# A float32 encoder layer on one core: its FFN from two token halves with paired down products to an up phase over all tokens and a down phase

## The chip, the core and the metric

One core of a Trainium2 chip runs the whole layer. The metric is the device time of one execution in microseconds. TensorE (PE) multiplies, VectorE (DVE), ScalarE (ACT) and GpSimd (POOL) work on tiles in SBUF, SyncE (SP) issues most DMAs.

## The reference, cut to what matters

Two inputs, 1024 and 256 tokens of width 1024, pass through the same layer; the kernel lays them one behind the other, T = 1280. Attention, a recurrent branch, a memory branch and their gates give `merged`; the part that the change touches begins there:

```python
x = x + merged @ w_out                       # part_out
h = rmsnorm(x, ffn_norm)
u = dwconv3(h @ w_up, ffn_conv) + ffn_conv_b # 1024 -> 2 x 2816, convolution of 3 tokens
u_val, u_gate = jnp.split(u, 2, axis=-1)
y = x + (jax.nn.silu(u_gate) * u_val) @ w_down   # 2816 -> 1024
return rmsnorm(y, final_norm)
```

`dwconv3` mixes each token with its two neighbours and takes zeros beyond the ends of each of the two inputs.

## The kernel before, in words

**Precision.** Every operand of the large products is split in two: a high half, cast on ACT (L182), and a low half, the difference, taken on DVE or POOL (L183). A product is three matmul passes, high by high, low by high, high by low.

**Projection.** `part_merge` writes `merged` transposed into the tile `hT`; `part_out` multiplies it with w_out tile by tile (ten tiles of 128 tokens), adds x (L1197), takes the norm (L233 to L253), scales (L1145, `xn`), transposes on TensorE (L1148) and keeps the result, transposed, as the FFN's input. The first five tiles' sums stay in SBUF (`acc`), the last five go to DRAM (`X2`, `XT`).

**FFN.** It runs over two halves of 640 tokens. Within a half the loop is over f, 22 blocks of 128 hidden columns; block f has a value part and a gate part. `products` (L1483) computes both parts by one level of Strassen's scheme, seven products in place of eight: the two parts by the two halves of the 1024 input rows by two token pieces of 322 columns. `ffn_weights` (L1344) makes the seven weight operands of an f: four raw blocks of w_up come by DMA (`wraw`), POOL forms sums (L1360, L1361, L1385, L1391), and `put` splits each into `fw`; it goes through all 22 f twice, once per half. Each product is 12 matmuls (L1520); its evacuation adds PSUM to earlier pieces (L1498 to L1510) and builds `fz`. `act` (L1527) then does the convolution: the centre tap on ACT (L1535), four side taps per half on DVE (L1542), Tanh on ACT, the gate step on DVE (L1547), the product on POOL (L1548), and splits the result into `fah` and `fal` (L1555, L1558). After every second f, `down` (L1560) multiplies two f with four pieces of w_down: ten PSUM tiles of six matmuls (L1574), each added by DVE into `acc` (L1565). `down_weights` splits w_down on POOL, for each half again. `finish` takes the last norm and stores. Operands of the second half are prepared during the first (`ffn_second`, `ffn_operands(1)`).

The order is written by hand: `hook(j)` after each product takes steps of the generators, and `in_order` (L1204) chains the instructions of PE, DVE, ACT and POOL in the order of the program within the FFN. The waiting chains are therefore those of the text:

```python
for f in range(22):
    products(half, f, hook)                 # 7 products of 12 matmuls, 322 columns
    if f % 2 and 3 <= f < 21:
        down(half, lambda t: act_steps(1))  # 10 tiles of 6 matmuls, 512 columns
```

PSUM has four buffers for up products (`psd`) and four for down products (`psw`). SP issues the loads in its own order; X2, XT and BT are stored from ACT's queue.

Of the kernel before, what the change touches and what calls it, by code (L numbers as in the profile page):

```python
# [32 lines left out]
AHEAD = 7  # L33

ACT_AFTER, DOWN_AFTER, BEHIND_AFTER = (1, 3, 5, 6), (0, 1, 5, 6), ((1, 3, 5), (1, 4))
ACT_STEPS = (2, 1, 1, 2, 2, 2, 1, 1, 1, 1)

SCALE_COLS = (1024,) * 5 + (0, 0, 512, 1024, 768)
# [28 lines left out]

CUT = 640

HALF = 322  # L70
IN_ORDER = (mybir.EngineType.PE, mybir.EngineType.DVE, mybir.EngineType.Activation, mybir.EngineType.Pool)

MTOK = (TOK, TOK, tuple((t, 320) for t in range(0, T, 320)))
# [81 lines left out]
class Builder:  # L155
# [136 lines left out]
    def build(self):  # L292
# [3 lines left out]
        with ExitStack() as ctx:  # L296
# [26 lines left out]
            mt, first = self.part_merge(mx)  # L323
            self.accp = ctx.enter_context(self.pool("acc"))

            self.acc = [self.accp.tile([128, D], F32, tag="acc", name="acc", bufs=5) for i in range(5)] + [None] * 5
            self.X2 = [None] * 5 + [self.dr.tile([128, D], F32, name="X2_%d" % i) for i in range(5, 10)]

            self.xp = ctx.enter_context(self.pool("xk"))
            self.zb = [self.xp.tile([128, 646], F32, name="fz%d" % i) for i in range(4)]  # L330
            self.xk = self.zb + [self.xp.tile([128, 646], F32, tag=t, name="xk", bufs=1) for t in ("fu0", "fu1", "fth")]
            self.xk.append(self.xp.tile([128, D], F32, tag="gain", name="xk", bufs=1))
            self.edge = self.xp.tile([128, 8, 2], F32, name="fedge")
            self.XT = self.dr.tile([128, 8, 640], F32, name="XT")
            self.BT = self.dr.tile([128, 28, HALF], F32, name="BT")
            self.raw_pool(ctx, "w", 5)

            self.fd = [self.H[:, c:c + 1024].rearrange("p (i n) -> p i n", i=2) for c in (0, 1024)]
            cols = [2048 + HALF * n for n in range(25)] + [8 * T + HALF * n for n in range(31)]
            b = [self.H[:, c:c + HALF] for c in cols]  # L340
            self.B = [[b[8 * j + 2 * k:8 * j + 2 * k + 2] for k in range(4)] for j in range(7)]
            self.W = []
            self.weights = self.ffn_weights()
            self.operands = self.ffn_operands(0)
            with wx, mx:
                self.part_out(mt, first)
            self.part_ffn()
# [715 lines left out]
    def part_merge(self, mx):  # L1063

        nc, a, dr = self.nc, self.ins, self.dr
        with self.pool("mg") as pool, self.pool("psm", 6, space=PSUM) as self.psd, ExitStack() as rx:
# [4 lines left out]
            mt = [[[self.H[:, c:c + CUT] for c in range(8 * CUT * i, 8 * CUT * (i + 1), CUT)] for i in (u, u + 1)] for u in (0, 2)]  # L1071
# [13 lines left out]
            def branch(n, m, o):  # L1085
# [4 lines left out]
                def evac(ps, t0, w):  # L1090
# [7 lines left out]
                    if n == 2:  # L1098
                        u, c = (0, t0) if t0 < CUT else (1, t0 - CUT)
                        h, l = mt[u][0][m][:, c:c + w], mt[u][1][m][:, c:c + w]  # L1100
# [19 lines left out]
        return mt, wh  # L1120
# [12 lines left out]
    def part_out(self, mt, first):  # L1133

        nc, a, pool = self.nc, self.ins, self.wo
        with self.pool("pso2", 2, space=PSUM) as psp, self.pool("psx", 2, space=PSUM) as pst, ExitStack() as rx:
            tmp = rx.enter_context(self.pool("ot"))
            new = lambda name: tmp.tile([128, D], F32, tag=name, name=name, bufs=1)
            ws = first + [self.out_rows(k, pool, "o%d" % k, 1) for k in range(2, 8)]

            def turn(i, x, junk):
# [7 lines left out]
                w = 128 if i < 5 else 2  # L1149
                if i < 6:  # L1150

                    for k in range(8):
                        for t0, t1, d in ((0, HALF, 0), (642 - HALF, 642, 2)):
# [30 lines left out]
            for i in range(10):  # L1184
# [4 lines left out]
                if i == 7:  # L1189
                    next(self.weights)  # L1190
# [489 lines left out]
```

## Time and profile before

| what | value |
|---|---|
| runs, median (lowest to highest) | 3241.52 us (3240.58 to 3250.91), 3 runs |
| the profiled execution | 3230.12 us, span 3227.9 us |
| mean granted TensorE clock | 0.958 |
| PE, DVE, ACT, POOL busy in the span | 2981.7, 2252.6, 1364.2, 1439.7 us |
| the FFN's last matmul, last instruction | 3216, 3227.9 us |

Busy times of engines overlap each other and are means over all stages; a busy PE also counts pipelined matmuls, so its dense pace is read from the starts of neighbouring matmuls. "PEclk" is the clock granted to TensorE as a share of the full one.

### The profile page before, as it was taken

The numbers are of one execution on the slowest core, as the hardware profiler recorded it, in microseconds if no ns is written. First come the engines' busy times: TensorE is split into PE (matmuls) and PEld (weight loads), VectorE is DVE, ScalarE is ACT, GpSimd is POOL, SyncE is SP. The second block draws the span as 40 slices with busy tenths as digits, with TensorE's granted clock in tenths as the row PEclk, the third lists the DMA queues.
The fourth block names the chain that finished last, engine by engine and source line by source line (L and its number), as shares of the span: only waits on it lengthen the run. The fifth ranks groups of instructions, "written<-read, shape, count | busy, mean of one in ns | idle before, by whom it ended". The sixth has DMA issues, their size and how long they took to land. (4 is left out here: it accounts for less than half of the span.)

```text
span 3227.9 us, 50384 instructions
## 1 busy us (share of the span) xinstructions
PE 2981.7 (92%) x18164; PEld 2509.7 (78%) x18164; DVE 2252.6 (70%) x4304; ACT 1364.2 (42%) x2995; POOL 1439.7 (45%) x1467
## 2 busy tenths in 40 slices
PE   7999999999989998999899999998899898789997
PEld 6778777777767777788777888987788888788886
DVE  5233488877887888844455414747888888988987
ACT  6232344544444544534555410333344345433344
POOL 2000266655666666731221000014676667566764
PEclk9999888988998999999999999999999999899999
DMA  6333312221222312226666335523232223312221
GB/s 225 110 117 110 128 60 66 71 69 61 79 71 68 92 55 66 63 85 167 170 195 174 115 137 192 179 81 126 92 111 82 86 74 134 130 63 79 79 76 52
DMA packets 204751, 338.09 MB, mean 105 GB/s; under 512 B 45987, under 2 KB 91811, under 8 KB 204503
## 3 DMA queue, kind: packets, MB, share of 16 engines
q1 hardware_dynamic: 194550, 325.02, 31.5%
q10 hardware_dynamic: 9952, 9.86, 0.9%
q8 instruction: 143, 2.34, 0.3%
q14 instruction: 106, 0.86, 0.1%
HBM read 244.47 MB, written 94.27 MB: 105 GB/s over the span
## 5 line engine op out<-in xcount | busy, mean ns | idle before, releaser
L205 PE MATMUL ps_d<-hT,whi 128*128 128x512 f32 (+1 forms) x2688 | 691.6, 382 | 1.6 <-ACT gt L822 1.4
L1520 PE MATMUL ps_d<-hT,fw 128*128 128x322 f32 x3672 | 564.3, 314 | 36.9 <-DVE fz L1498 21.5
L1520 PEld LDWEIGHTS ps_d<-hT,fw 128*128 128x128 f32 x3672 | 554.4, 191 | 46.6 <-DVE fz L1498 22.1
L205 PEld LDWEIGHTS ps_d<-hT,whi 128*128 128x128 f32 x2688 | 452.1, 195 | 64.0 <-issue 6.2
L205 PE MATMUL ps_d<-hT,wlo 128*128 128x512 f32 (+1 forms) x1344 | 356.3, 381 | 0.0
L648 POOL TENSOR_TENSOR Lk<-Lh,c_lev 128x512 f16<-128x512 f16 x200 | 241.1, 1208 | 138.3 <-PE ps_y L651 135.4
L183 DVE TENSOR_TENSOR wlo<-wraw,whi 128x512 fp32r<-128x512 f32 x152 | 117.2, 782 | 193.2 <-ACT whi L182 192.3
L205 PEld LDWEIGHTS ps_d<-hT,wlo 128*128 128x128 f32 x1344 | 227.9, 196 | 28.5 <-issue 2.5
L183 DVE TENSOR_TENSOR fw<-wraw,fw 128x512 fp32r<-128x512 f32 x174 | 214.1, 1245 | 40.0 <-ACT fw L182 39.5
L1542 DVE SCALAR_TENSOR_TENSOR fu<-fz,fconv,fu 128x640 f32<-128x640 f32 (+1 forms) x176 | 206.0, 1171 | 26.9 <-ACT fu L1535 26.9
L1574 PE MATMUL ps_dn<-hT,fah 128*128 128x512 f32 x420 | 150.8, 426 | 63.5 <-DVE acc L1565 63.3
L653 ACT CAST Yl<-ps_y 128x512 f16<-128x512 f32 x200 | 117.0, 585 | 135.6 <-PE ps_y L651 134.8
L1548 POOL TENSOR_TENSOR fu<-fu 128x640 f32<-128x640 f32 (+1 forms) x44 | 70.1, 1593 | 217.9 <-DVE fu L1547 217.1
L183 POOL TENSOR_TENSOR hT<-xk,hT 128x322 fp32r<-128x322 f32 x4 | 4.1, 1058 | 360.8 <-DVE xn L1145 360.0
L658 ACT CAST X<-ps_x 128x512 f16<-128x512 f32 x200 | 116.8, 585 | 103.9 <-PE ps_x L656 98.4
L1574 PE MATMUL ps_dn<-fdw,fah 128*128 128x512 f32 x460 | 155.9, 411 | 3.7 <-DVE acc L1565 3.6
L1574 PEld LDWEIGHTS ps_dn<-hT,fah 128*128 128x128 f32 x420 | 84.0, 200 | 90.7 <-DVE acc L1565 71.2
L1565 DVE TENSOR_TENSOR acc<-acc,ps_dn 128x512 f32<-128x512 f32 x220 | 145.8, 678 | 3.2 <-PE ps_dn L1574 3.2
L182 ACT CAST fw<-sum 128x512 fp32r<-128x512 f32 x132 | 78.4, 619 | 157.4 <-POOL sum L1391 84.8
L182 ACT CAST whi<-wraw 128x512 fp32r<-128x512 f32 x152 | 91.3, 620 | 121.2 <-PE ps_d L205 118.1
L183 DVE TENSOR_TENSOR fw<-sum,fw 128x512 fp32r<-128x512 f32 x90 | 115.0, 1277 | 36.8 <-ACT fw L182 36.5
L205 PE MATMUL ps_d<-bo,whi 128*128 128x320 f32 (+2 forms) x640 | 127.2, 337 | 4.1 <-DMA bo<-O 3.3
(359 smaller groups left out, 6812.0 us busy)
## 6 DMA issues: line engine op xcount, KB each, us to landing
wraw<-in_w_up SPq DMA_DIRECT2D x176, 256.0 KB, 2.6
wraw<-in_w_in SPq DMA_DIRECT2D x112, 256.0 KB, 3.0
draw<-in_w_down SPq DMA_DIRECT2D x88, 256.0 KB, 2.6
kr<-RKV SPq DMA_DIRECT2D x40, 384.0 KB, 3.3
bo<-O SPq DMA_DIRECT2D x24, 640.0 KB, 8.7
gate<-GT SPq DMA_DIRECT2D x20, 640.0 KB, 4.1
R<-VR SPq DMA_DIRECT2D x40, 256.0 KB, 2.7
GT<-gt SPq DMA_DIRECT2D x40, 256.0 KB, 2.2
```

The lines of the kernel that those rows point to most:

```text
L182: nc.scalar.copy(hi, src)
L183: (eng or nc.vector).tensor_sub(lo, src, hi.bitcast(F32))
L205: nc.tensor.matmul(ps[:, :n], lhsT=w[:, k, :], rhs=x[k][:, t0:t0 + n], start=i == 0, stop=i == 3 * kt - 1)
L648: nc.gpsimd.tensor_mul(Lk, Lh, bc(self.lev[:, d, l, :]))
L653: nc.scalar.copy(Yl, py)
L658: nc.scalar.copy(f(X2), f(px))
L1520: nc.tensor.matmul(ps, lhsT=w[:, u, 128 * k:128 * k + 128], rhs=B[j][k][v], start=n == 0, stop=n == 11)
L1542: nc.vector.scalar_tensor_tensor(o[:, :m], in0=z[j][:, lo_c + d:hi_c + d], scalar=fc[:, blk, i:i + 1], in1=o[:, :m], op0=ALU.mult, op1=ALU ...
L1548: nc.gpsimd.tensor_mul(val[:, :m], val[:, :m], gt[:, :m])
L1565: nc.vector.tensor_add(s, s, ps)
L1574: nc.tensor.matmul(ps, lhsT=x[f][u][:, 128 * i:128 * i + 128], rhs=w[:, v], start=n == 0, stop=n == 5)
```

## The change

The FFN becomes two phases. **Up phase** (`ffn_up`): for f from 0 to 21 the seven products run over all 1280 tokens. The two token pieces of Strassen's scheme are now the tokens 0 to 639 and 640 to 1279, so that no piece needs a halo; each product runs in two slots, z = 0 with 384 and z = 1 with 256 columns of each (`PARTS`). The weights of an f are prepared once. Evacuation goes straight into `z`, one buffer for value and gate of all tokens (in the tile `X0`, with `th`); the centre and side taps, the gate steps and the product run on two parts of 640 and 642 columns into four tiles `fu` (in `X2K`). The product is stored to DRAM (`AD`), not split. **Down phase** (`ffn_down`): for 20 units, ten tiles of tokens by two halves of the output columns, the activation of the tile is loaded from `AD` and split (`a_load`, `a_split`), and 66 matmuls over all f add up in one PSUM bank; one DVE addition with x takes it out. The 22 w_down pieces of the first column half are split at the end of the up phase into room that the operands leave, those of the second half while the tenth unit runs. The first two units run in segments (f below 11, to 20, and 21), since f = 21 is stored and loaded last.

`part_out` keeps no sums in SBUF: all ten tiles go to `X2`, the order of tiles is 0, 1, 2, 5, 6, 7, 3, 4, 8, 9, so that the operands of z = 0 are complete first, and DVE scales the transposed tile in one instruction in place of eight or sixteen on ACT. `part_merge` cuts its last branch into 384 and 256 columns, where it had 320.

The diff, cut:

```diff
-AHEAD = 7
-ACT_AFTER, DOWN_AFTER, BEHIND_AFTER = (1, 3, 5, 6), (0, 1, 5, 6), ((1, 3, 5), (1, 4))
+PARTS = ((0, 384), (384, 256))
+FIRST = ((0, 0), (1, 0), (2, 0), (3, 0), (0, 1), (4, 0), (1, 1), (5, 0), (2, 1), (6, 0), (3, 1), (4, 1), (5, 1), (6, 1))
+PUT_AFTER = (0, 4, 6, 8, 9, 11, 12)
+ACT_AFTER = (1, 2, 4, 5, 7, 8, 9, 10, 12)
+F_GROUPS = ((0, 11), (11, 10), (21, 1))
...
-            self.psd = cx.enter_context(self.pool("psf", 4, space=PSUM))
-            self.psw = cx.enter_context(self.pool("psw", 4, space=PSUM))
+            self.psd = px.enter_context(self.pool("psf", 8, space=PSUM))
...
         def put(x):
-            w = self.fd[len(self.W)] if first else self.big([128, 2, 512], F32R, "fw")
-            self.split(w[:, 0], w[:, 1], fl(x), nc.gpsimd if put.n % 7 == 5 and put.n > 14 else None)
+            w = self.fw[put.n % len(self.fw)]
+            self.split(w[:, 0], w[:, 1], fl(x), nc.gpsimd if put.n % 7 in (2, 6) else None)
...
+        def out(f, j, c, ps):
+            add = lambda o, y: nc.vector.tensor_add(o, ps, y)
...
+            if j == 0:
+                nc.scalar.copy(p1, ps)
+            elif j == 1:
+                add(q, p1)
...
+            elif j == 4:
+                add(g1, v1)
+                add(g0, q)
...
+            centre(0, 0, vals[0])
+            centre(0, 1, vals[1])
+            sides(0, 0, vals[0])
+            yield
+            sides(0, 1, vals[1])
+            centre(1, 0, gts[0])
+            yield "value"
...
+            gate(0, 1)
+            times(0)
+            tanh(1, 0)
+            yield
+            gate(1, 0)
+            tanh(1, 1)
+            store(0)
+            yield
...
+        for f in range(1, 22):
+            for n in range(14):
+                j, c = divmod(n, 2)
+                if c == 0:
+                    w = self.W.pop(0)
+                slot(f, j, c, w)
+                if f < 21 and n in PUT_AFTER or f == 21 and n in (0, 4, 6):
+                    weight()
+                if f == 21 and c == 1 and n > 1:
+                    next(down)
+                    next(down)
+                if n in ACT_AFTER:
+                    act_step()
+                while len(late) > 1:
+                    evac()
...
+            def second(f):
+                self.split(wd[f][:, 0], wd[f][:, 1], y[2][f % 3], nc.gpsimd if f % 3 == 2 else None)
+                load_second(f + 3)
...
+                for f in range(f0, f1):
+                    g, i = divmod(f, 11)
+                    hi, lo = [x[:, 128 * i:128 * i + 128] for x in self.aset[t % 2][g]]
+                    for m, (u, v) in enumerate(((hi, 0), (lo, 0), (hi, 1))):
+                        nc.tensor.matmul(ps[n], lhsT=u, rhs=wd[f][:, v], start=f == 0 and m == 0, stop=f == 21 and m == 2)
```

**Where instructions move.** First DVE in the steady FFN (L183 a weight's low half, L1498 to L1510 evacuations, L1542 side taps, L1547 a gate step, L1558 the activation's low half, L1565 a down tile's addition). Before, a piece of one half:

```order
L1547 SCALAR_TENSOR_TENSOR fu<-fth,fu 128x642
L1510 TENSOR_TENSOR ft_23392<-ps_d,ft_23390 128x322
L183 TENSOR_TENSOR fw<-sum,fw 128x512
L1502 TENSOR_TENSOR ft_23394<-ps_d,ft_23392 128x322
L183 TENSOR_TENSOR fw<-wraw,fw 128x512
L1505 TENSOR_TENSOR ft_23393<-ps_d,ft_23392 128x322
L1558 TENSOR_TENSOR fal<-fu,fah 128x384
L1558 TENSOR_TENSOR fal<-fu,fah 128x256
```

Now, a piece of one f of the up phase (L1340 evacuations, L1374 side taps, L1387 gate steps; xk_22445 holds `z` and `th`, xk_22447 the `fu` tiles):

```order
L1374 SCALAR_TENSOR_TENSOR xk_22447<-xk_22445,fconv,xk_22447 128x640 x2
L1374 SCALAR_TENSOR_TENSOR xk_22447<-xk_22445,fconv,xk_22447 128x642 x2
L1340 TENSOR_TENSOR xk_22447<-ps_d,xk_22447 128x384
L183 TENSOR_TENSOR fw_23318<-sum,fw_23318 128x512
L1374 SCALAR_TENSOR_TENSOR xk_22447<-xk_22445,fconv,xk_22447 128x640 x2
L1340 TENSOR_TENSOR xk_22447<-ps_d,xk_22447 128x256
L1374 SCALAR_TENSOR_TENSOR xk_22447<-xk_22445,fconv,xk_22447 128x642 x2
L1340 TENSOR_TENSOR xk_22445<-ps_d,xk_22447 128x384
L1340 TENSOR_TENSOR xk_22445<-ps_d,xk_22447 128x256
L1387 SCALAR_TENSOR_TENSOR xk_22447<-xk_22445,xk_22447 128x320
```

The activation's low half and the additions of down tiles are gone from between the evacuations; eight side taps and four gate steps of an f stand between its 14 evacuations.

Second PE at the step from the projection to the FFN (L1148 and L1153 transposes of a scaled tile `xn`, L1178 and L1167 the projection). Before:

```order
L1178 MATMUL ps_w<-woh,hT 128x512 x4
L1178 MATMUL ps_w<-wol,hT 128x512 x2
L1148 MATMUL ps_x_23357<-c_ident,xn 128x128 x8
L1520 MATMUL ps_d<-hT 128x322 x24
L1520 MATMUL ps_d<-hT,fw 128x322 x108
L1305 MATMUL ps_x_23701<-c_ident,fx 128x128 x4
```

Now:

```order
L1167 MATMUL ps_w<-woh,hT 128x512 x4
L1167 MATMUL ps_w<-wol,hT 128x512 x2
L1153 MATMUL ps_x_23260<-c_ident,xn 128x128 x8
L1153 MATMUL ps_x_23292<-c_ident,xn 128x128 x8
L1470 MATMUL ps_d<-hT,fw_23311 128x384 x12
L1470 MATMUL ps_d<-hT,fw_23318 128x384 x12
```

The transposes of the last tile stood behind 132 up matmuls (L1305); now they stand ahead of the first.

Third SP between the two phases (L1399 to L1402 stores of the activation of f = 21, L1317 loads of activations, L1575 loads of x):

```order
L1399 DMA AD_21_22438<-xk_22447 128x640
L1401 DMA AD_21_22441<-xk_22447 128x384
L1402 DMA AD_21_22441<-xk_22447 128x256
L1317 DMA h2T<-AD_21_22438 128x128 x2
L1564 DMA fgain<-in_final_norm 128x1024
L1575 DMA fx_29050<-X_0_22426 128x512
L1575 DMA fx_29051<-X_1_22427 128x512
L1317 DMA h2T<-AD_0_22436 128x1408
L1317 DMA h2T<-AD_11_22437 128x1280
```

The loads of the third tile (the last two rows) stand behind the stores of f = 21 and the loads of what was stored; nothing of this was there before.

## Rows read from the trace of the kernel before

**Rows 1.** The page, busy time and share of the span by engine.
```profile
PE 2981.7 (92%) x18164; PEld 2509.7 (78%) x18164; DVE 2252.6 (70%) x4304; ACT 1364.2 (42%) x2995; POOL 1439.7 (45%) x1467
```

**Rows 2.** Stretches: length, busy us (instructions) PE, PEld, DVE, ACT, POOL, PEclk, DMA share, GB/s.
```profile
2084.00:2202.50 118.50, 117.36 (x552) 97.28 (x551) 53.92 (x103) 41.73 (x114) 17.29 (x23) 1.00 0.33 109
2278.00:2656.00 378.00, 341.65 (x1888) 310.16 (x1888) 318.02 (x389) 148.14 (x251) 250.94 (x171) 0.96 0.27 88
...
2760.00:3160.00 400.00, 358.81 (x1993) 328.16 (x1994) 358.92 (x467) 162.74 (x292) 252.31 (x178) 0.95 0.24 79
...
3216.00:3228.00 12.00, 0.00 (x0) 0.00 (x0) 6.79 (x18) 2.78 (x6) 3.31 (x3) 0.61 0.43 175
2870.89:2914.41 43.52, 40.61 (x238) 37.28 (x237) 39.20 (x51) 18.34 (x34) 28.57 (x21) 1.00 0.23 73
```

**Rows 3.** Timeline of PE in dense stretches: start us, length us, line, shape, count.
```profile
237.17 1.12 PE L205 MATMUL ps_d<-hT,wlo 128*128 128x256 f32 x8
238.13 1.12 PE L205 MATMUL ps_d<-hT,whi 128*128 128x256 f32 x8
...
2061.13 1.33 PE L205 MATMUL ps_d<-bo,whi 128*128 128x320 f32 x8
2062.30 0.75 PE L205 MATMUL ps_d<-bo,wlo 128*128 128x320 f32 x4
...
2102.34 1.07 PE L1178 MATMUL ps_w<-woh,hT 128*128 128x512 f32 x4
2103.25 0.61 PE L1178 MATMUL ps_w<-wol,hT 128*128 128x512 f32 x2
2103.70 1.07 PE L1178 MATMUL ps_w<-woh,hT 128*128 128x512 f32 x4
```

**Rows 4.** Single lines in the FFN: count, duration ns min/median/max, first and last start.
```profile
L183 DVE TENSOR_TENSOR fw<-wraw,fw x174: 673/1372/1940, 2212.3 to 3173.0; 128x512 fp32r<-128x512 f32 x174
L1542 DVE SCALAR_TENSOR_TENSOR fu<-fz,fconv,fu x176: 868/883/1929, 2238.1 to 3197.7; 128x640 f32<-128x640 f32 x88, 128x642 f32<-128x642 f32 x88
L1565 DVE TENSOR_TENSOR acc<-acc,ps_dn x220: 671/678/689, 2285.8 to 3218.7; 128x512 f32<-128x512 f32 x110
L1520 PEld LDWEIGHTS ps_d<-hT,fw x3672: 186/188/338, 2208.2 to 3184.6; 128*128 128x128 f32 x194
```

**Rows 5.** Groups by form in the FFN, DVE: count, busy us, mean ns, idle before.
```profile
L183 DVE TENSOR_TENSOR fw<-wraw,fw 128x512 fp32r<-128x512 f32 x174 | 214.1, 1245 | 40.0 <-ACT fw L182 39.5
L1542 DVE SCALAR_TENSOR_TENSOR fu<-fz,fconv,fu 128x642 f32<-128x642 f32 x88 | 104.2, 1185 | 12.7 <-ACT fu L1535 12.7
L1498 DVE TENSOR_TENSOR fz<-ps_d,ft 128x322 f32<-128x322 f32 x88 | 42.3, 480 | 2.2 <-PE ps_d L1520 2.1
L1498 DVE TENSOR_TENSOR fz<-ps_d,ft 128x256 f32<-128x256 f32 x22 | 9.0, 408 | 0.0
```

**Rows 6.** Timeline of DVE, two neighbours in the steady state.
```profile
2895.28 0.68 DVE L1565 TENSOR_TENSOR acc<-acc,ps_dn 128x512 f32<-128x512 f32 x1
2895.88 0.88 DVE L1542 SCALAR_TENSOR_TENSOR fu<-fz,fconv,fu 128x642 f32<-128x642 f32 x1
```

**Rows 7.** POOL in the FFN, two groups by form and one single line.
```profile
L1391 POOL TENSOR_TENSOR sum<-wraw,sum 128x512 f32<-128x512 f32 x44 | 73.0, 1660 | 21.9 <-DVE fw L183 21.9
L1548 POOL TENSOR_TENSOR fu<-fu 128x642 f32<-128x642 f32 x22 | 35.1, 1594 | 112.6 <-DVE fu L1547 111.8 <-DVE fm L243 0.8
L183 POOL TENSOR_TENSOR fw<-sum,fw x42: 1285/1296/1782, 2242.1 to 3172.7; 128x512 fp32r<-128x512 f32 x42
```

**Rows 8.** Timeline of DVE at the projection's end, one tile's addition and scaling.
```profile
2192.53 1.22 DVE L1197 TENSOR_TENSOR x<-x,ps_w 128x1024 f32<-128x1024 f32 x1 [3.62 <-DMA x<-in_x_sample]
2199.39 0.75 DVE L1145 TENSOR_SCALAR xn<-x,fr 128x1024 f32<-128x1024 f32 x1
```

**Rows 9.** w_down in the FFN: its loads (KB, us to landing) and its casts on ACT.
```profile
draw<-in_w_down SPq DMA_DIRECT2D x88, 256.0 KB, 2.6
L182 ACT CAST fdw<-draw 128x512 fp32r<-128x512 f32 x46 | 28.4, 617 | 8.5 <-DMA draw<-in_w_down 8.5
```

More of the change, by code (lines that the diff above doesn't have):

```diff
@@ L322, in build @@
             mx = ExitStack()
[L323 to L344, printed above, removed]
-            with wx, mx:
-                self.part_out(mt, first)
-            self.part_ffn()
+            first = self.part_merge(mx)
@@ new lines, in build @@
+            rows = lambda x, n: x.rearrange("p (k w) -> p k w", k=8)
+            self.xz = [[rows(self.X0, n0), rows(x1, n0)], [rows(self.X2K[:, 8 * n1 * u:8 * n1 * u + 8 * n1], n1) for u in range(2)]]
+            self.raw_pool(ux, "w", 5)
+            with wx, mx:
+                self.part_out(first)
+            h2 = ctx.enter_context(self.pool("h2", side="right"))
+            self.H2 = h2.tile([128, 15360], F32R, name="h2T")
+            self.fw = [h2.tile([128, 2, 512], F32R, name="fw0")]
@@ L349, in rwkv_consts, with merged @@
+            self.part_ffn(ux)
+    def merged(self, part, k, t0, n):
+        u, r = divmod(t0, 640)
+        z = r >= PARTS[1][0]
+        t, w = PARTS[z]
+        c = 32 * t + (8 * part + k) * 2 * w + u * w + r - t
+        return self.H[:, c:c + n]
     def rwkv_consts(self):
@@ L1131, in out_rows, with part_out @@
         return h, l
-    def part_out(self, mt, first):
+    def part_out(self, first):
         nc, a, pool = self.nc, self.ins, self.wo
@@ L1414, in slot @@
             while late:
                 late.pop(0)()
-            late.append(ev)
-        def act_steps(n):
-            for _ in range(n):
-                while acts and next(acts[0], "end") == "end":
-                    acts.pop(0)
-        def down_weights():
-            fd = self.fd + [pool.tile([128, 2, 512], F32R, name="fdw%d" % i) for i in range(2)]
-            order = [(h, f + i, c) for h in range(2) for f in range(0, 22, 2) for c in range(2) for i in range(2)]
-            raws = []
-            def load(n):
-                if n < len(order):
-                    _, f, c = order[n]
-                    raws.append(self.draw[n % 2])
-                    nc.sync.dma_start(raws[-1], a["w_down"][f][:, 512 * c:512 * c + 512])
-            load(0)
-            load(1)
-            for n, (h, f, c) in enumerate(order):
-                if h == 1 and f >= 20:
-                    w = self.big([128, 2, 512], F32R, "fdw")
-                else:
-                    w = fd[n % 4]
-                self.split(w[:, 0], w[:, 1], raws.pop(0), nc.gpsimd)
-                W2.append(w)
-                load(n + 2)
-                yield
@@ L1560, in down @@
-        def down(half, hook, whole=False):
-            x = [A.pop(0) for _ in range(2)]
-            def add(s, ps):
-                nc.vector.tensor_add(s, s, ps)
-            for t, (i, c) in enumerate([(i, c) for i in range(5) for c in range(2)] if whole else
-                                       [(i, c) for c in range(2) for i in range(5)]):
-                ps = self.psw.tile([128, 512], F32, tag="w", name="ps_dn")
-                n = 0
-                for f in range(2):
-                    w = W2[2 * c + f]
-                    for u, v in ((0, 0), (1, 0), (0, 1)):
-                        nc.tensor.matmul(ps, lhsT=x[f][u][:, 128 * i:128 * i + 128], rhs=w[:, v], start=n == 0, stop=n == 5)
-                        n += 1
-                slot(lambda s=self.acc[5 * half + i][:, 512 * c:512 * c + 512], p=ps: add(s, p))
-                hook(t)
-            del W2[:4]
@@ L1652, in ffn @@
-        for _ in bg:
-            pass
 _INS = ["x_prompt", "x_sample", "mem_prompt", "mem_sample", "attn_norm", "w_in", "na_rpb", "rw_conv", "rw_decay0",
```

677 lines of the change are left out of this document (346 added, 331 removed).

## The prediction

> **What bounds the kernel now.** I read the whole-span line first. TensorE is busy for 92% and VectorE for 70% [rows 1]; but that is a mean over stages, and the change touches only the last third. So the second view is the table of busy times by stretch [rows 2]. The projection `part_out` ends at 2202.5 us and the FFN takes the rest, 3227.9 - 2202.5 = 1025.4 us. In the FFN's two steady stretches TensorE is busy for 342 of 378 us and 359 of 400, VectorE for 318 and 359, and the granted clock is 0.96 and 0.95, where the projection before it had 1.00.
>
> Third, what would TensorE need if nothing held it? The starts of its matmuls in dense stretches give the price of one [rows 3]: 512 columns, six in 1.36 us, 226.7 ns; 320 columns, eight in 1.17 us, 146 ns; 256 columns, eight in 0.96 us, 120 ns. That is columns divided by 2.4 GHz plus some 13.3 ns in each case. The FFN before has 2 x 22 x 7 x 12 = 3696 up matmuls of 322 columns (147.5 ns each, 545.2 us) and 2 x 11 x 10 x 6 = 1320 down matmuls of 512 (299.2 us): 844.4 us. So 181 us of the FFN's 1025.4 is not matmul time.
>
> Where it goes is seen in one period of the steady state, two f and one `down`, the last line of [rows 2]: 43.52 us, against 24.8 + 13.6 = 38.4 us of matmuls. VectorE is busy for 39.2 of it and POOL for 28.6. The view of single lines shows how these two hinder each other [rows 4]. A VectorE subtraction that reads two SBUF tiles (the low half of an up weight, L183) takes 673 ns at best and 1372 in the median; L1542 (the convolution's side taps) 868 at best and 1929 at worst. An addition with a PSUM operand, L1565, never leaves 671 to 689. So VectorE's work on SBUF alone takes about twice as long at times, and POOL is the engine that is then at work beside it. The steady period is set by VectorE and POOL together, not by TensorE.
>
> **The change, part by part.** *TensorE.* The Strassen products now pair the tokens 0 to 639 with 640 to 1279, and each product runs over 384 and then 256 columns: 22 x 7 x 12 = 1848 matmuls of each width, at 173.3 (384 / 2.4 + 13.3) and 120 ns. That is 24.64 us per f and 542.0 us in all. The down matmuls stay 1320 of 512 columns, 299.2 us. The sum is 841.2 us against 844.4: TensorE itself gains nothing.
>
> *VectorE, up phase, per f (both token halves).* Removed: the up weights are prepared once instead of twice, 7 splits per f fewer; the activation's split (L1558) leaves this phase; the 220 `acc` additions of 678 ns go, with 20 evacuations at the end in their place. What stays, in mean durations [rows 5]: 14 PSUM evacuations, seven at 256 columns (0.41 us) and seven at 384 (0.55, one step beyond the 0.48 of 322 columns), 6.7 us; 8 side taps x 1.185 = 9.5; 4 gate steps of half that width, 0.6 each, 2.4; 5 weight subtractions x 1.245 = 6.2 (two more are POOL's). Sum 24.8 us. That would be level with TensorE's 24.64, but two things lower it. Neighbours overlap: an addition shown as 0.68 us is followed after 0.60 [rows 6], so 31 instructions give back 2.5 and leave 22.3. And POOL has less to do: four sums x 1.66, two subtractions x 1.30 and two products x 1.594 [rows 7] make 12.4 us per f, 50% of the time, where it was 28.6 of 43.5, 66%. With POOL idle the best durations give 6.7 + 8 x 0.87 + 4 x 0.44 + 5 x 0.67 = 18.8, less the overlap 16.3. Between 16.3 and 22.3 I take 21, nearer to what runs today. That is below 24.64, so TensorE becomes the bound, with eight PSUM buffers as slack; in VectorE's new order the side taps and gate steps stand spread between evacuations, so that a late one delays only its neighbours. For ripples I take 0.5 us per f, 10 us; bounds 0 and 54 (the first rival).
>
> *Moved to the down phase.* Each tile's activation is loaded and split there, 18 times 2816 columns: 5.5 times a 512-column piece of 0.62 us on ACT [rows 9] and 0.67 on VectorE, 3.4 and 3.7 us per tile, beside 66 matmuls, 15.0 us. Covered; without that cover it would be 18 x 7 us. The w_down splits fall from 88 to 44. At the ninth and tenth tile 22 of them pass through three buffers for the second column half: a round is a load, 2.6 us, a copy, 0.62 [rows 9], and a subtraction, 0.7 to 1.7, so 1.3 to 1.6 us per weight and 29 to 36 us in all, where TensorE passes the two tiles in 29.9. I take 5 us, bounds 0 and 12.
>
> *Start.* TensorE now transposes the last tile of the projection ahead of any up product. From a tile's addition to the end of its scaling the same chain took 2192.53 to 2200.14, 7.6 us [rows 8]; I take 6 us of idle time, bounds 5 and 8. Then four products of z = 0 (8.3 us) must cover the operand splits of z = 1. Ahead of the first of these VectorE has the transposed data (1.2 us), three splits of 1536 columns (5.4), three weights (1.8) and the split itself (1.2), after 1 us of transposes: 10.6 us at best, and about 29 for the whole first f against 24.64. I take 10 us, bounds 4 and 16.
>
> *Between the phases.* Behind the last up product VectorE still has the last gate steps, three splits and the rest of w_down. In SP's order the load of the third tile stands behind the store of f = 21, which waits for POOL. TensorE's cover is 126 matmuls, 28.6 us. I take 12 us, bounds 2 and 20; what is late next is the split of the third tile.
>
> *End.* After the last matmul 12 us were left [rows 2]; the rest is now half as wide. I take 10, bounds 8 and 12. For a clock below full in the stalls I take 4 us, bounds 0 and 20 (half of what 0.95 would cost over 841 us).
>
> **Sum.** 841.2 + 6 + 10 + 10 + 12 + 5 + 10 + 4 = 898 us in place of 1025.4: 127 us less. The profiled execution took 3230.1 us, 2.2 more than its span, and the median of the runs is 3241.5, 11.4 above it. Against the profile's own time the forecast is 3103, at the median's level **3114 us**.
>
> **The rivals.** *First: VectorE and POOL stay the bound in the up phase.* If nothing of their work overlaps, VectorE's 16.3 us and POOL's 10.9 at best (six of 1.29, two of 1.59) stand one behind the other: 27.2 us per f, 2.6 over TensorE, 21 x 2.6 = 54 us instead of 10: 3158. For it: 21 of 24.64 us is 85%, near the 90% at which VectorE is the bound now. Against it: PSUM evacuations keep their width whatever POOL does [rows 4]. The Trainium skill, page "SBUF — State Buffer", section "Who interferes with whom", states that a Vector instruction with two SBUF inputs and a GpSimd instruction that reads SBUF exclude each other for a whole instruction; with the evacuations free of that, its rule would give 27.2 - 5.6 = 21.6 us per f and leave the forecast as it is, and the widths in rows 4 agree with it.
>
> *Second: the weight load sets the pace of narrow products.* If a 256-column matmul could not start sooner than a weight load is shown busy, 188 ns in the median [rows 4], 1848 x 68 ns = 126 us would come back: 3240, no change. The eight 256-column matmuls in 0.96 us speak against it, though that stretch is short.
>
> *Third, slower: VectorE runs at its longest durations throughout.* Place: the up phase, in which z, the `fu` tiles and `th` have one buffer each, so that the evacuation of the third product queues behind the side taps of the f before. With side taps at 1.93, weight subtractions at 1.94 and gate steps at 0.97 us [rows 4], an f takes 15.4 + 9.7 + 3.9 + 6.7 - 2.5 = 33.2 us, 8.1 over my 25.1, so 21 x 8.1 = 170 us: 3284. It is slower than before from 31.1 us per f on (127 / 21 = 6.0 more than mine). Against it: POOL would have to be at work beside every such step, and it has 12.4 us of work per f.
>
> **How the numbers follow.** Forecast 0.74, first rival 0.17, second 0.03, third 0.06. Range: at the lower end the stalls at their lower bounds, 841.2 + 5 + 4 + 0 + 2 + 0 + 8 + 0 = 860, 38 us below mine, 3076; at the upper end past the first rival, 3176. Left out are the other two rivals and the corner where several terms reach their upper bounds at once. A measurement of this kernel can tell some 0.3% from no change. Faster: forecast and first rival, 0.91; same: the second and what lies around it, 0.04; slower: the third, with what little remains, 0.05.
>
> **What would show it.** Right: in the middle of the up phase an f takes 24.6 to 25.5 us, TensorE is dense, the granted clock is 1.00 and VectorE below 90%; a tile of the down phase takes 15.0 us. Wrong: if TensorE waits for VectorE in every f, the first rival; if 256-column matmuls start more than 130 ns apart, the second; if VectorE's side taps have a median near 1.9 us, the third. The sum also fails if TensorE stands still for over 20 us between the last up product and the third down tile.

## The result and the profile after

The changed kernel took 3091.2 us in the median of four runs (3087.6 to 3099.3), the kernel before, on the same chip, 3245.0 us (3240.6 to 3250.9): a ratio of 0.953, 95% interval 0.950 to 0.956, 154 us less. The forecast was 127 us less, at 3114, in a range from 3076 to 3176. The profiled execution took 3087.6 us, 142 below the one before, where the forecast on that basis was 3103.

The page's line of busy times, against [rows 1]: VectorE and POOL fell by 306 and 357 us, TensorE by 52.

```profile
PE 2929.3 (95%) x18164; PEld 2477.7 (80%) x18164; DVE 1946.3 (63%) x4001; ACT 1242.3 (40%) x2693; POOL 1082.5 (35%) x1186
```

The stretches of the FFN, with the columns of [rows 2]: four short ones behind stalls, the swap of w_down, the steady up phase and two pieces of the down phase.

```profile
2213.50:2216.40 2.90, 2.90 (x11) 2.90 (x10) 1.22 (x1) 0.00 (x0) 2.45 (x2) 0.50 0.14 31
2233.50:2236.80 3.30, 3.30 (x10) 3.10 (x11) 3.30 (x6) 1.34 (x2) 0.41 (x1) 0.50 0.24 78
2762.80:2766.20 3.40, 3.40 (x8) 2.74 (x9) 3.40 (x4) 3.25 (x4) 1.02 (x1) 0.51 0.97 311
2790.20:2796.20 6.00, 5.69 (x13) 4.00 (x14) 1.87 (x3) 0.48 (x2) 0.00 (x0) 0.50 0.95 319
2932.00:2943.00 11.00, 7.23 (x28) 4.44 (x27) 3.93 (x6) 4.33 (x7) 3.23 (x3) 1.00 0.37 122
2260.00:2740.00 480.00, 480.00 (x3330) 480.00 (x3329) 399.94 (x620) 192.92 (x339) 239.05 (x160) 1.00 0.22 72
2800.00:2915.00 115.00, 115.00 (x506) 94.67 (x505) 33.85 (x28) 27.81 (x37) 13.12 (x10) 1.00 0.39 127
2945.00:3075.00 130.00, 130.00 (x571) 106.97 (x570) 45.25 (x87) 36.17 (x51) 0.27 (x1) 1.00 0.39 131
```

Where [rows 2] showed TensorE busy for 342 of 378 us, it is now busy for 480 of 480 at a clock of 1.00, with VectorE at 83%. The 3330 matmuls in 480 us make 144.1 ns each; at 168 per f that is 24.2 us. VectorE is busy for 400 / 480 x 24.2 = 20.2 us of it, POOL for 12.1.

The seams, in the timeline of PE (start us, length us, line, shape, count, idle time before and what ended it), and from the chain of waits the piece without a gap:

```profile
2212.48 1.30 PE L1153 MATMUL ps_x<-c_ident,xn 128*128 128x128 f32 x8 [3.98 <-DVE xn L1150]
2213.44 8.29 PE L1470 MATMUL ps_d<-hT,fw 128*128 128x384 f32 x36
...
2233.43 4.04 PE L1470 MATMUL ps_d<-h2T,fwx 128*128 128x384 f32 x12 [5.43 <-ACT fwx L182]
...
2251.22 1.04 PE L1470 MATMUL ps_d<-hT,fw 128*128 128x384 f32 x5
```
```profile
2242.86 497.91 PE ps_d L1470 x3454
```
```profile
2762.72 21.15 PE L1660 MATMUL ps_d<-hT,h2T 128*128 128x512 f32 x85 [1.99 <-DVE h2T L183]
2784.63 1.66 PE L1660 MATMUL ps_d<-hT,h2T 128*128 128x512 f32 x6 [0.76 <-POOL hT L183]
2788.93 0.50 PE L1660 MATMUL ps_d<-hT,h2T 128*128 128x512 f32 x1 [2.64 <-POOL hT L183]
...
2790.19 0.79 PE L1660 MATMUL ps_d<-h2T 128*128 128x512 f32 x1 [0.30 <-POOL h2T L183]
```

The terms of the sum, each from such starts:

| term | forecast, us | measured, us |
|---|---|---|
| projection's last matmul to first up product | 6 | 6.2 |
| first f | 24.6 + 10 | 37.8 |
| f = 1 to 21, ripples included | 21 x 24.64 + 10 = 527.4 | 509.1 |
| first 132 down matmuls | 29.9 + 12 | 41.9 |
| the other 18 units, swap included | 269.3 + 5 | 105.4 + 35.3 + 135.3 = 276.0 |
| end | 10 | 7.6 |
| clock in stalls | 4 | within the lines above, about 8: half of the 15.6 us at a clock of 0.50 |
| FFN | 898 | 878.6 |

The FFN is 146.8 us shorter than its 1025.4 (147.2 when both are read from the start of the projection's last matmul, which makes it 1025.8 before). The projection ended 4.7 us later in this execution than in the one before, and the profile's time is 1.7 over its span instead of 2.2: -146.8 + 4.7 - 0.5 makes the 142 us. Against the medians there are 8 more, since the profiled execution before was 11.4 below its median and this one 3.6.

### The profile page after: what moved, and what is told of

Same layout as the page of the kernel before. It is cut to its first block, busy times and chain, and to the rows that moved or that the text cites. A ratio compares the mean times of both kernels' runs of the same rounds, so it can differ in the third digit from the quotient of the medians.

```text
span 3085.9 us, 49265 instructions
## 1 busy us (share of the span) xinstructions
PE 2929.3 (95%) x18164; PEld 2477.7 (80%) x18164; DVE 1946.3 (63%) x4001; ACT 1242.3 (40%) x2693; POOL 1082.5 (35%) x1186
## 4 chain that ended last, share of the span: by engine, by line
PE 75%; DVE 10%; POOL 6%; issue 3%; ACT 3%; DMA 2%; SPq 0%; ACTq 0%; POOLq 0%; DVEq 0%
PE ps_d L205 26%; PE ps_d L1470 16%; PE ps_d L1660 9%; PE ps_w L1167 3%; PE ps_o L945 3%; PE ps_c L722 2%; PE ps_c L707 2%; PE ps_y L653 1%; PE ps_gO L611 1%; PE ps_pt L863 1%; PE ps_x L658 1%; DVE X L661 1%; PE ps_gE L608 1%; PE ps_c L710 1%; PE ps_bt L628 1%
## 5 line engine op out<-in xcount | busy, mean ns | idle before, releaser
L1660 PE MATMUL ps_d<-hT,h2T 128*128 128x512 f32 x1110 | 275.4, 394 | 7.3 <-POOL hT L183 4.1
L1660 PEld LDWEIGHTS ps_d<-hT,h2T 128*128 128x128 f32 x1110 | 210.5, 190 | 54.5 <-POOL hT L183 5.3
L183 DVE TENSOR_TENSOR wlo<-wraw,whi 128x512 fp32r<-128x512 f32 x152 | 117.1, 781 | 192.9 <-ACT whi L182 192.0
L1374 DVE SCALAR_TENSOR_TENSOR xk<-xk,fconv,xk 128x642 f32<-128x642 f32 (+1 forms) x176 | 178.7, 1026 | 3.1
L1470 PE MATMUL ps_d<-hT,fwx 128*128 128x256 f32 (+1 forms) x1080 | 159.0, 306 | 2.2 <-ACT fwx L182 1.6
L1470 PEld LDWEIGHTS ps_d<-hT,fwx 128*128 128x128 f32 x1080 | 156.5, 188 | 2.9 <-ACT fwx L182 1.9
L1470 PE MATMUL ps_d<-hT,fw 128*128 128x256 f32 (+1 forms) x1032 | 156.1, 310 | 0.6 <-ACT hT L182 0.6
L1340 DVE TENSOR_TENSOR xk<-ps_d,xk 128x256 f32<-128x256 f32 (+1 forms) x308 | 140.6, 480 | 22.1 <-PE ps_d L1470 21.8
L1470 PEld LDWEIGHTS ps_d<-hT,fw 128*128 128x128 f32 x1032 | 153.2, 190 | 1.6 <-ACT hT L182 0.9
L205 PE MATMUL ps_d<-bo,whi 128*128 128x256 f32 (+2 forms) x640 | 127.0, 337 | 4.2 <-DMA bo<-O 3.1
L1470 PE MATMUL ps_d<-h2T,fw 128*128 128x384 f32 (+1 forms) x840 | 125.4, 308 | 0.0
```

Source lines behind the costliest of these rows:

```text
L183: (eng or nc.vector).tensor_sub(lo, src, hi.bitcast(F32))
L205: nc.tensor.matmul(ps[:, :n], lhsT=w[:, k, :], rhs=x[k][:, t0:t0 + n], start=i == 0, stop=i == 3 * kt - 1)
L1340: add = lambda o, y: nc.vector.tensor_add(o, ps, y)
L1374: nc.vector.scalar_tensor_tensor(o[:, :m], in0=z[j][:, lo + d:lo + d + m], scalar=fc[:, f + 22 * j, i:i + 1], in1=o[:, :m], op0=ALU.mult, ...
L1470: nc.tensor.matmul(ps, lhsT=w[:, u, 128 * k:128 * k + 128], rhs=B[c][j][v][:, k], start=n == 0, stop=n == 11)
L1660: nc.tensor.matmul(ps[n], lhsT=u, rhs=wd[f][:, v], start=f == 0 and m == 0, stop=f == 21 and m == 2)
```

## The experiments

The question is why TensorE's stalls went. The theory on record is that VectorE and POOL set the period before and no longer do; the first rival is that order, buffers or product widths did it. Times of single runs stand against 3091.2 (changed) or the 3243.3 that the kernel before took beside them. They also hold the part ahead of the FFN, whose last matmul started anywhere from 2190.7 to 2226.0 us in these executions, though its instructions are the same. So the length of the FFN itself, from that start to the end of the span, stands beside each of them, against 1025.8 us before and 878.6 changed.

**The additions, taken out of the kernel before.**

```diff
-                nc.vector.tensor_add(s, s, ps)
+                nc.vector.tensor_add(s[:, :m], s[:, :m], ps[:, :m])
...
-                    down(half, lambda t: act_steps(1))
+                    down(half, lambda t: act_steps(1), m=32)
```

> The kernel before, with the additions of 18 of its 22 downs (all but the last two of each half) cut from 512 to 32 columns; most of the partial sums are left out, so its output is not the reference's. It keeps the halves, the two preparations of the up weights and four PSUM buffers. Theory (VectorE, together with POOL, set the steady period before): ten additions of 0.68 us leave each pair of f, about 5 us of VectorE's 39, and the pair falls from 45.1 us (first half) and 43.9 us (second half) to between TensorE's 38.5 and 40.5; 60 to 100 us less in all. Rival (the stalls came from the order of the work, with chains over several engines and four PSUM buffers, whatever VectorE's share): the pair stays within 1 us and the time within 20 us.

3196.5 us, 47 less (FFN 986.7, 39 less). The starts of the downs lie 42.6 us apart in the first half and 41.6 in the second (45.1 and 43.9 before). The second half, in stretches:

```profile
2750.00:3120.00 370.00, 347.36 (x1961) 319.95 (x1962) 305.93 (x453) 157.64 (x281) 249.20 (x177) 0.96 0.25 85
```

VectorE is down from 90% to 83% and TensorE still isn't dense: VectorE lost its 5 us per pair, the period only half of that. The result lies between the numbers of the two theories; VectorE's total alone is not what bounds the pair.

**One preparation of the up weights, in the kernel before.**

```diff
-            self.split(w[:, 0], w[:, 1], fl(x), nc.gpsimd if put.n % 7 == 5 and put.n > 14 else None)
+            if put.n < 154:
+                self.split(w[:, 0], w[:, 1], fl(x), nc.gpsimd if put.n % 7 == 5 and put.n > 14 else None)
+            else:
+                nc.scalar.copy(w[:, 0], fl(x))
+                nc.scalar.copy(w[:, 1], fl(x))
```

The four sums on POOL (L1360, L1361, L1385, L1391) are left out there too.

> The kernel before, with the second half's up weights no longer prepared on VectorE and POOL: no sums and differences, and the low half of each weight is a plain copy by ACT; this part of the computation is left out. The first half is untouched and serves as the control. Theory: in the second half about 15 us of VectorE's 39 and 14 us of POOL's 29 leave each pair, and the pair falls from 43.9 to 38.5 to 39.5 us, where TensorE is the bound; about 50 us less in all, more than the additions alone give in one half. If POOL's stretching of VectorE is what mattered, side taps fall to a mean below 1 us in the second half. Rival (order and PSUM buffers): pair within 1 us of 43.9.

3169.9 us, 73 less (FFN 958.6, 67 less). The stretches of the first and the second half, and VectorE's side taps in the second:

```profile
2290.00:2660.00 370.00, 336.13 (x1855) 305.03 (x1854) 312.62 (x381) 144.31 (x244) 247.45 (x169) 0.95 0.28 89
2750.00:3120.00 370.00, 367.07 (x2169) 343.13 (x2168) 217.29 (x382) 246.06 (x457) 111.19 (x99) 1.00 0.28 92
```
```profile
L1548 DVE SCALAR_TENSOR_TENSOR fu<-fz,fconv,fu 128x642 f32<-128x642 f32 x68 | 61.1, 899 | 11.1 <-ACT fu L1541 11.0
```

In the first half nothing moved. In the second, nine pairs in a row take 38.8 us each, TensorE dense at a clock of 1.00, with four PSUM buffers and the old order; the change of halves gives another 21 us. Side taps fall from 1185 ns [rows 5] to 899. So the order of the kernel before was able to keep TensorE busy; the preparation on VectorE and POOL was in the way.

**Both edits.**

> The kernel before with both edits: the additions of 18 downs cut to 32 columns and the second half's up weights not prepared on VectorE and POOL (both parts of the computation left out). Theory: TensorE's matmuls are the floor, so the second half's pair stands at 38.5 to 39, no lower than with the preparation alone left out, and the first half's as with the additions alone; 80 to 120 us less in all. What is then still missing to the changed kernel (154 us less) lies at the start, at the change of halves and at the end. Rival (the gain needs the two phases themselves): less than 60 us.

3131.8 us, 111.5 less (FFN 939.3, 86 less). The second half's pairs stay at 38.8, the first half's are at 42.5: as the theory has it, TensorE is the floor where the preparation is gone.

**The additions put back into the changed kernel.**

```diff
             elif j == 2:
-                add(v1, q)
+                [add(v1, q) for _ in range(3 - c if 1 <= f < 21 else 1)]
```

The same stands at j = 1, 3 and 4.

> The changed kernel with 15 PSUM evacuations of f = 1 to 20 repeated (ten of 384 columns, five of 256; the output is the same): about 6.4 us more VectorE work per f, for the 6.0 us of additions that the change took out of the steady work. VectorE was at 20.2 of 24.24 us per f. Theory (VectorE's work per f is what decides, with 4 us of slack now): an f takes 26 to 27.5 us and VectorE is over 95% busy; 40 to 65 us more. Rival (the gain is from the new order, the wider products and the eight PSUM buffers, and VectorE's work overlaps more than its busy time tells): an f stays below 25 us, under 15 us more.

3183.3 us, 92 more (FFN 987.4, 109 more), in the sense of the theory and beyond its numbers:

```profile
2300.00:2800.00 500.00, 442.94 (x2860) 437.31 (x2860) 465.89 (x783) 161.45 (x289) 205.24 (x137) 0.95 0.19 59
```

```profile
PE ps_d L1471 <- DVE xk L1340: 57.1, 33, 2.7
```

The second row is from the waits (us in total, times, longest): TensorE stood for 57 us behind L1340. 2860 matmuls are 17 f, so an f takes 29.4 us. VectorE's busy time went up by 7.2 us to 27.4, not by 6.4, and it filled 93% of the time, not all of it: in its own order it waits for casts of late weights. The changed kernel's headroom is thus 0.93 x 24.2 - 20.2 = 2.3 us per f.

**POOL's four sums twice, in two places.** The extra work is eight additions of 248 columns. In the first run four stand behind the sums of L1278 and L1279 and four ahead of those of L1300 and L1301; in the second all eight stand behind L1301.

```diff
             nc.gpsimd.tensor_sub(fl(s2), fl(a12), fl(s2))
+            for i in range(8 if put.n >= 7 else 0):
+                nc.gpsimd.tensor_add(self.xj, fl(a21)[:, :248], fl(a22)[:, :248])
```

> The changed kernel with eight more additions of 248 columns on POOL for each f (their result is not used; the output is the same), in place of the four sums and differences of 512 that the second preparation cost: POOL from 12.1 to about 17.5 us per f, VectorE's own work as it was. Theory (both engines work at once and POOL only stretches VectorE's SBUF work, by 3.1 us per f now, 15.3 against 12.1 at its shortest durations): the stretch grows with POOL's time to about 4.5 us, VectorE goes from 20.2 to 21 to 22.5 us and stays below TensorE's 24.24; 0 to 15 us more. Rival (the two never work side by side on SBUF, so their shortest times add up: 12.1 and 16.1 make 28.2 us per f): some 80 us more. A second rival, that POOL does not touch VectorE at all: VectorE stays at 20.2.

> The changed kernel with the same eight extra POOL additions for each f as in the run with the sums twice, but all eight behind the last of POOL's four sums, where POOL stood idle for 8.3 us, so that no weight is later for them. First theory (new, after the run with the sums twice took 28.0 us per f where the shortest durations of VectorE's SBUF work and POOL's work sum to 12.1 + 16.1 = 28.2: the two never work on SBUF side by side, and the longer records are waiting): an f takes 27 to 28.5 us wherever POOL's work is put; 60 to 85 us more. Second theory (that run was slow because the extra work stood ahead of sums that VectorE's queue then waited for): an f takes 24.2 to 25 us, 0 to 15 us more.

3167.9 us (77 more, FFN 84 more, 28.0 us per f) and 3142.0 us (51 more, FFN 57 more, 26.6 us per f): the first came where the rival had put it and far over my 0 to 15; the second lies 9 us under the lower end of "one at a time" (3 us by the FFN) and far over the other theory. First run and second run:

```profile
2300.00:2700.00 400.00, 359.75 (x2407) 350.06 (x2406) 302.37 (x446) 135.57 (x243) 270.15 (x231) 1.00 0.20 62
```
```profile
2300.00:2700.00 400.00, 372.39 (x2530) 367.40 (x2528) 343.17 (x466) 142.56 (x256) 315.40 (x240) 1.00 0.21 65
```

The first has two causes mixed: VectorE idles for 24%, most of it behind weights that POOL's queue now makes late, as at this place in its timeline:

```profile
2508.69 1.13 DVE L183 TENSOR_TENSOR fw<-wraw,fw 128x512 fp32r<-128x512 f32 x1 [5.37 <-ACT fw L182]
```

The second separates them: 1.4 of the 3.8 us were the place, 2.4 remain where no sum comes later for them. How they arise is seen where VectorE's four side taps meet the extra additions, in the timelines of the second run (VectorE, then POOL), and of the run with the additions put back, where POOL was idle at that place:

```profile
2521.05 4.80 DVE L1377 SCALAR_TENSOR_TENSOR xk<-xk,fconv,xk 128x640 f32<-128x640 f32 x4
```
```profile
2520.20 8.62 POOL L1303 TENSOR_TENSOR xk<-wraw 128x248 f32<-128x248 f32 x7
```
```profile
2508.56 3.51 DVE L1375 SCALAR_TENSOR_TENSOR xk<-xk,fconv,xk 128x640 f32<-128x640 f32 x4
```

A side tap that takes 0.88 us alone and an addition that takes 0.72 at its shortest run in step at 1.2 us a pair: about halfway between full overlap (0.88 us) and taking turns (1.6 us). The Trainium skill, page "SBUF — State Buffer", section "Who interferes with whom", calls it an exclusive lock for a whole instruction; by the strict rule both runs would stand at 28.2 us (28.8 with the 0.72 us of an addition, for which the expectation had counted 0.65). The direction agrees, the 26.6 of the second run is below it: the records hold some 0.4 us per pair that does overlap.

**The preparation twice, in the changed kernel**: each split repeated, and POOL's eight additions as in the first of the two runs above.

```diff
-            self.split(w[:, 0], w[:, 1], fl(x), nc.gpsimd if put.n % 7 in (2, 6) else None)
+            [nc.scalar.copy(w[:, 0], fl(x)) for _ in range(2)]
+            [e.tensor_sub(w[:, 1], fl(x), w[:, 0].bitcast(F32)) for _ in range(2)]
```

`e` is the engine that did it before; f = 0 is as it was.

> The changed kernel with each up weight of f = 1 to 21 split twice (same values; five more subtractions on VectorE, two more on POOL, seven more copies on ACT for each f) and the eight extra POOL additions: the preparation that the change took out, put back. Theory: VectorE goes from 20.2 to 25.5 to 28 us per f, which is more than TensorE's 24.24, and since the run with the additions put back filled VectorE only to 93%, an f takes 27 to 30 us; 55 to 120 us more, about what leaving the preparation out of one half of the kernel before gave back (73 us) or up to half as much again. Rival (the order is what counts): under 15 us.

3336.8 us, 246 more (FFN 1109.0, 230 more), about twice the upper end: an f takes 33.5 to 36.6 us, 35.0 in the mean.

```profile
2300.00:2700.00 400.00, 322.25 (x1914) 309.05 (x1913) 290.57 (x411) 156.61 (x272) 246.94 (x210) 0.90 0.16 49
```

VectorE's 25.4 us per f are the lower end of what was expected, yet it is busy for 73% only, and POOL for 62%; I had counted VectorE's queue alone. Turns on SBUF count both: VectorE's shortest durations of SBUF work, 12.1 + 5 x 0.67, and POOL's, 16.1 + 2 x 1.29, make 34.2 (34.7 with 0.72 us per addition). The misplaced additions are in this run too, so not all of it is turns.

**POOL's weight steps on VectorE.**

```diff
-            nc.gpsimd.tensor_add(fl(s1), fl(a21), fl(a22))
+            nc.vector.tensor_add(fl(s1), fl(a21), fl(a22))
```

So for the other three sums and for both splits.

> The changed kernel with POOL's six weight steps of each f (four sums and differences, two subtractions) on VectorE; POOL keeps the two products. First theory (one at a time on SBUF): six steps of 0.67 us come to VectorE's 16.3 us of shortest durations and POOL's 7.7 us leave the shared time, so VectorE's busy time stays at 20 to 22 us per f, though it now does six steps more, and its subtractions and side taps fall to within 0.15 us of their shortest durations; TensorE stays the bound, within 10 us of the changed kernel. Second theory (side by side, POOL stretching VectorE a little): VectorE goes from 20.2 to 23 to 24.5 us, with its ceiling at 93%, and an f takes 25 to 26.3 us; 15 to 45 us more.

3085.4 us, 6 less (FFN 880.2, 2 more). Steady stretch, and the single side taps of this run and of the changed kernel (ns min/median/max, first and last start):

```profile
2300.00:2700.00 400.00, 400.00 (x2775) 400.00 (x2774) 369.83 (x614) 160.37 (x284) 50.99 (x33) 1.00 0.23 71
```
```profile
L1374 DVE SCALAR_TENSOR_TENSOR xk<-xk,fconv,xk x136: 867/883/891, 2300.1 to 2693.0; 128x640 f32<-128x640 f32 x68, 128x642 f32<-128x642 f32 x68
```
```profile
L1374 DVE SCALAR_TENSOR_TENSOR xk<-xk,fconv,xk x160: 868/883/1981, 2259.4 to 2739.7; 128x642 f32<-128x642 f32 x80, 128x640 f32<-128x640 f32 x80
```

POOL lost 9 us of work per f, VectorE gained six steps of 0.68 us, and its busy time rose by only 2.2, to 22.4 us (20 to 22 expected); TensorE did not notice. No side tap is longer than 0.89 us now; those up to 1.98 came from POOL's work beside them. In the subtractions from sums, beside which POOL's products now stand, some waiting is left (1144 and 1089 ns in the mean).

**Four PSUM buffers in place of eight** in the changed kernel.

> The changed kernel with four PSUM buffers in place of eight, as the kernel before had. Theory (VectorE has some 2 us per f to spare, so a late evacuation is made good at once): an f grows by less than 0.5 us, 0 to 10 us in all, most of it in the first f. Rival (the eight buffers are what took the ripples of the steady state away): an f takes 25 to 27 us, 20 to 60 us more, with TensorE waiting for L1340.

3083.6 us, 8 less, but an FFN of 884.5, 6 more: every f from 1 to 20 takes 24.2 us as with eight, the last 25.0. Most of the difference is at the start: from the projection's last matmul to the second f 48.6 us instead of 44.0. So the buffers are not the cause; nor are the wider products, since the 322 columns of the kernel before ran dense without the preparation.

**The seams mended**, in two versions; the second has POOL's early subtraction on VectorE instead.

```diff
-                y[2] = [pool.tile([128, 512], F32, name="draw%d" % i) for i in range(3)]
+                y[2] = [pool.tile([128, 512], F32, name="draw%d" % i) for i in range(6)]
...
-FIRST = ((0, 0), (1, 0), (2, 0), (3, 0), (0, 1), (4, 0), (1, 1), (5, 0), (2, 1), (6, 0), (3, 1), (4, 1), (5, 1), (6, 1))
+FIRST = ((0, 0), (1, 0), (2, 0), (3, 0), (0, 1), (4, 0), (5, 0), (1, 1), (6, 0), (2, 1), (3, 1), (4, 1), (5, 1), (6, 1))
...
-                if f == 21 and n == 12:
+                if f == 21 and n == 11:
                     self.a_split(0, 0, H[:, 9216:10624])
```

The split of the third piece stands ahead of that step's w_down splits.

> The changed kernel with three seams mended. Six buffers in place of three for the second half of w_down, loaded four matmul groups earlier; in the first f the subtraction on POOL for z = 1 is issued ahead, the weights of the fifth and sixth product are prepared ahead of the operands and the sixth product of z = 0 goes ahead of the second of z = 1; between the phases the first tile's split goes ahead of the last w_down splits, and two of those move from POOL to VectorE. Theory (each of these seams costs what the profile shows: 5.4 us at the swap, 13.5 in the first f, 11.9 between the phases): 0 to 1 us left at the swap, 6 to 10 in the first f, 4 to 9 between the phases; 8 to 18 us below the changed kernel, a ratio to the kernel before of 0.946 to 0.951. Rival (a stall mended only uncovers the next one, for VectorE is late by then): less than 4 us.

> As the run with three seams mended, but in the first f the two subtractions for z = 1 that POOL did are on VectorE, in their old place. In that run the one on POOL, issued early, stretched VectorE's three splits beside it from 5.1 to 7.3 us and the third product's weight came 2 us later. First theory (one at a time on SBUF, 1.2 us on VectorE for 2.3 on POOL): the first f loses 6 to 10 us instead of 13.5, the swap none, the stretch between the phases 9 to 10, so the FFN takes 862 to 870 us where the changed kernel takes 878.6; 9 to 16 us less in all, which the medians of the runs may barely tell. Second theory (the next wait takes its place): FFN above 872.

> The changed kernel once more, beside the mended one on the same chip, with nothing altered. Its ratio to the kernel before should lie in 0.950 to 0.956 again, and its FFN take 876 to 882 us in the trace; the mended kernel should lie below it by 9 to 16 us by the first theory, by less than 5 by the second.

The first version: 3092.0 us in the median, ratio 0.956 (0.951 to 0.960), no gain in the times; its FFN took 874.2 us. The swap is gone (30.4 us for two units, 35.3 before), the stretch between the phases 39.6 instead of 41.9, but the first f 39.7 instead of 37.8: POOL's early subtraction met VectorE's splits. VectorE and POOL in this version, and VectorE in the changed kernel, where POOL stood idle beside it:

```profile
2211.60 7.30 DVE L183 TENSOR_TENSOR h2T<-xk,h2T 128x1536 fp32r<-128x1536 f32 x3
```
```profile
2211.50 2.45 POOL L1218 TENSOR_TENSOR xk<-xk 128x1024 f32<-128x1024 f32 x1
```
```profile
2219.16 5.08 DVE L183 TENSOR_TENSOR h2T<-xk,h2T 128x1536 fp32r<-128x1536 f32 x3
```

Three splits took 2.2 us longer, nearly the whole length of POOL's one instruction.

The second version: 3082.1 us, ratio 0.951 (0.948 to 0.954); the changed kernel beside it 3100.0, ratio 0.957 (0.955 to 0.959), just above the 0.950 to 0.956 expected of it. The mended version's median lies below those of both kernels. But its FFN takes 873.6 us against 880.4, not the 862 to 870 forecast: the first f is still at 38.6, one late weight having taken the place of another. So 7 of the 18 us are shown in the FFN. The rest lies ahead of it, where both kernels run the same instructions and where executions of one kernel differ as well: the projection's last matmul came at 2195.4 us here, and at 2207.2 and 2217.8 in two executions of the changed kernel. I don't claim those 11 us.

## Why the prediction was right, step by step

**The bound.** That VectorE and POOL held TensorE up is shown from both sides: without the preparation the kernel before runs at TensorE's pace; with more work on either engine the changed one falls behind it. "VectorE and POOL together" was the better half of the sentence. The additions gave back only 2.3 to 2.5 of the 5 us that they take of VectorE per pair; they read PSUM and leave the turns on SBUF as they were. The preparation gave back all that TensorE's floor lets through.

The count of turns also fits the kernel before. These lines have shortest records that [rows 4] and [rows 7] lack:

```profile
L1547 DVE SCALAR_TENSOR_TENSOR fu<-fth,fu x44: 810/818/1931, 2250.5 to 3198.5; 128x640 f32<-128x640 f32 x22, 128x642 f32<-128x642 f32 x22
L1558 DVE TENSOR_TENSOR fal<-fu,fah x66: 410/560/1907, 2257.8 to 3202.1; 128x640 fp32r<-128x640 f32 x22, 128x384 fp32r<-128x384 f32 x22, 128x256 fp32r<-128x256 f32 x22
L1498 POOL TENSOR_TENSOR fz<-ft,ft x66: 325/878/1477, 2224.7 to 3185.9; 128x320 f32<-128x320 f32 x22, 128x64 f32<-128x64 f32 x22, 128x256 f32<-128x256 f32 x22
L183 POOL TENSOR_TENSOR hT<-draw,hT x42: 1266/1742/1881, 2250.0 to 3167.8; 128x512 fp32r<-128x512 f32 x42
```

With the shortest record of each line and width, the pair of 43.52 us in [rows 2] holds, as an estimate, 18.6 us of VectorE's instructions on SBUF alone (12 of 0.67, 8 of 0.87, 2 of 0.81, 4 of 0.41 and 0.54) and 23.0 of POOL's (14 of 1.26 to 1.29, 2 of 1.54, 4 of 0.33 and 0.74). That is 41.6 us, more than TensorE's 38.4 and nearly the whole pair. The additions are not in this sum, and without them the pair stood at 41.6 to 42.6.

**TensorE's floor** was mis-sized by 9 us. The forecast took 120 ns for 256 columns [rows 3]; in the steady up phase 384 columns start every 173.4 ns, as forecast, and 256 every 115.2, which makes the f of 24.24 us (84 of each). That takes 1848 x 5 ns off the 542, and puts the f just below the 24.6 to 25.5 us that the prediction named as its sign.

**VectorE's 21 us** came out at 20.2, POOL's 12.4 at 12.1. The **ripples** of 10 us, and the whole first rival, did not come: not one stall from 2251 to 2760. Yet the rival's mechanism exists. Its price was too high, because it put the PSUM evacuations into the same queue of turns; with VectorE's SBUF work alone the turns sum to 12.1 + 10.9 = 23.0 us, just under TensorE's 24.24. The Trainium skill's rule on the page "SBUF — State Buffer", section "Who interferes with whom", gave 21.6 in the prediction, with overlaps of neighbours taken off, and so TensorE as the bound, which is what came. What I had not seen is how thin that margin is: 5 to 6 us more of POOL's work per f use it up.

**Start, seams and end.** The handover was right; the first f lost 13.5 us over its 24.24, some 3 of them at half the clock, instead of 10; the stretch between the phases lost the 12 forecast, but that the number fits is in part luck. Of it 6.0 us are idle times, behind the splits of the activation (2.0 and 0.3 us) and of w_down (0.8, 2.6 and 0.3); 4.7 are what the half clock cost over 3.4 and 6.0 us, which the sum had as a term of its own. For the split of the third tile, which the prediction expected to be late next, TensorE did not wait. The swap lost 5.2 where 5 stood. The end took 7.6, below its lower bound of 8. The second and third rivals fell by the 115 ns and by side taps with a median of 0.883 us.

**The error**, 23 us at the median: 19 in the FFN (8 from the floor of f = 1 to 21, 10 from ripples, 2 from the end, 4 for a clock term that the other terms already held, less 3 for the first f and 2 for the down units), 4 back for the projection's end and the span, and 8 because the sum was carried to a median that lay 11.4 above its profile where the new one lies 3.6 above.

## What to carry to other kernels

Add up, for each period, VectorE's instructions that take all inputs from SBUF and POOL's, at their shortest durations, and compare the sum with what TensorE needs; here it was good to some 8%. Where it was above, the pair was the bound although neither engine looked full (41.6 against 38.4 us: 43.5 measured; 28.8 against 24.24: 26.6 and 28.0; 34.7 against 24.24: 35.0); where it was below (23.0 against 24.24), TensorE was. POOL takes 1.29 us for what VectorE does in 0.68, so moving work to POOL lengthens the sum and bringing it back to VectorE can cost nothing, as long as VectorE's own total leaves room. Instructions that read PSUM stand outside that sum, so cutting them can give back less than their busy time. A wide spread between the shortest and the longest record of one line is the sign to look for.

## What was not expected of the hardware

After idle times of 4.0, 5.4 and 2.0 us TensorE ran at a granted clock of 0.50 to 0.51, its lower level of 1.2 GHz (the first three stretches above, 2.9 to 3.4 us long; in the second some ten matmuls of 384 columns fill 3.3 us, where 1.7 are usual), and after idle times of 0.8, 2.6 and 0.3 us between 2783.9 and 2790.2 it ran at 0.50 for the 6.0 us that follow. But the stalls of the swap, idle times of 0.6 to 1.3 us between 2932 and 2943, left it at 1.00. And a 256-column matmul started every 115 ns although each has its own weight load with a record of 188 ns, 480 us long without a gap.
